# Normalisation split in two steps, a lagged mesh, and low weight parts made by accumulating DMAs

## The chip, the cores and the metric

One core of a Trainium2 chip runs the kernel. The metric is device microseconds of one execution. TensorE is called PE, VectorE DVE, ScalarE ACT, GpSimd POOL, and SyncE SP; SP issues all loads of the kernel before.

## The reference

Two transformer blocks over 512 tokens with a model width of 1024, in float32. Block 1 has two layers; block 2 has one, with a modulation computed from a vector c.

```python
for l in range(DEPTH):                                  # block 1, DEPTH = 2
    u = rmsnorm(x, norm_mix[l])
    proj = u @ w_in[l]
    q, k, v, iq, ik, iw, cB, cC, ch, g = jnp.split(proj, offsets, axis=-1)
    ...                                                 # rope on q, k, iq, ik
    y_attn = dsa_attention(q, k, v, iq, ik, iw) @ w_attn_out[l]
    y_conv = (cB * short_conv(cC * ch, conv_w[l])) @ w_conv_out[l]
    gates = jax.nn.sigmoid(g.reshape(B, T, N_BRANCH, D))
    merged = gates[:, :, 0] * y_attn + gates[:, :, 1] * y_conv
    x = x + merged @ w_mix_out[l]
    u = rmsnorm(x, norm_mlp[l])
    x = x + jnp.square(jax.nn.relu(u @ w_mlp_up[l])) @ w_mlp_down[l]
x = rmsnorm(x, norm_final)
mod = jax.nn.silu(c) @ w_ada[0] + b_ada[0]              # block 2
sh_m, sc_m, gt_m, sh_f, sc_f, gt_f = jnp.split(mod, N_MOD, axis=-1)
x = x + gt_m * token_mixer(modulate(rms_norm(x, g_mix), sh_m, sc_m), ...)
h = modulate(rms_norm(x, g_ffn), sh_f, sc_f)
x = x + gt_f * ((jax.nn.silu(h @ w_gate) * (h @ w_up)) @ w_down)
```

`dsa_attention` lets each query attend to the 128 keys of the highest index score; `token_mixer` joins a dilated attention with a chunkwise mLSTM.

## The kernel before, in words

Activations lie transposed, as eight tiles of 128 features by 512 tokens. Each float32 product is made of three float32r products: a value is split into a high part (`hi`) and the rest (`lo`), and hi x hi, hi x lo and lo x hi are summed in one PSUM bank. Activations are split by `hilo` and `prep`: ACT writes the high part, DVE subtracts it.

The program is a list of items that `Prog.run` walks in order. A "unit" is a piece of weights: 4 contraction tiles by 256 outputs (512 KB), or by 128 outputs where it is "narrow". Before the products of unit `cur` are emitted, the loads (`fetch`) of units up to `cur + early` (5) and the splits (`split`) of units up to `cur + ahead` (2) are emitted. `split` copies the raw weights to `wh` on ACT (L217) and subtracts into `wl` on DVE (L218); narrow units use slots of the general pool `gp` (62 of 128x512), the others four buffers of `whp`. There are eight raw buffers. "bg" items are background steps, taken out at a "rate" per unit, and "drain" empties them. The order in which each engine runs its instructions is set at build time and may differ a little from the order of the list.

`linear` makes products of 128 outputs by 512 tokens (L279 to L281), with `parts_=2` in two halves of 256 tokens. `linear_tok` makes V with the tokens as outputs (L430 to L432). `seven` makes a 2x2 block product in seven half-size products instead of eight (L401 to L403); it needs sums of weights (L327 to L336) and mixed activations `ta` and `tb`, which `mix` makes (L476 to L479, then `hilo` L455 and L456). `mesh` puts the pieces of one list between those of another, here the MLP's `down` of chunk c-1 between the `up` of chunk c.

A layer of block 1 runs: projections gC and gA, then V, q, k, H, B and the first gates, with the index scores and top-k (L795, L796) as background; `w_conv_out`; attention with the second gates; `w_attn_out`; `w_mix_out`, whose eviction `evmix` adds to x (L912), and prepares and squares the tile (L463, L464, L494, L495). The first MLP chunk u0 follows as a `linear`: after its second piece `rstd` sums the squares with a matrix of ones (L501), takes a root on ACT and a reciprocal on DVE over 128x512 (L503 to L505, `refine` L511 to L513), while four `mix` groups run as background; evictions are L928. Then the meshes follow, with c = 1 to 7, and the last `down`. Before the mixer, `norm` does the same `rstd` and `norm2` reduces its result to columns.

At the end of block 1 and before the FFN of block 2 the norm runs in column form, one half of the tokens after the other: `colsum` (L1045), a few instructions on two columns, `spread` (L1054 on DVE, L1056 on PE), and `hnorm` (L1066, L1076, L1079). The FFN begins with `gateup(0, 2)` and `gateup(1, 1)` in narrow units (L1533 to L1535).

Of the kernel before, what the change touches and what calls it, by code (L numbers as in the profile page):

```python
# [50 lines left out]
class Prog:  # L51
# [9 lines left out]
    def run(self):  # L61
        units = [p for k, p in self.items if k == "unit"]
        got = 0
        nxt = 0
        cur = 0
        bg = deque()
        rate = 1.0
        credit = 0.0
        for kind, pay in self.items:
            if kind == "unit":  # L70
                while got < len(units) and got <= cur + self.early:
                    self.fetch(units[got])
                    got += 1
                while nxt < len(units) and nxt <= cur + self.ahead:
                    self.split(units[nxt])
                    nxt += 1
                cur += 1
                credit += rate
                while credit >= 1.0:
                    credit -= 1.0  # L80
                    if bg:
                        bg.popleft()()
            elif kind == "do":
                pay()
            elif kind == "bg":
                bg.extend(pay)
            elif kind == "rate":
                rate = pay
            elif kind == "drain":
                while bg:  # L90
                    bg.popleft()()
# [18 lines left out]
def mesh(a, b):  # L110

    n = len(a)
    out = []
    for i, x in enumerate(a):
        out.extend(x)
        for p in b[i * len(b) // n : (i + 1) * len(b) // n]:
            out.extend(p)
    return out
# [3 lines left out]
def blocks_kernel(ctx: ExitStack, tc: tile.TileContext, a: dict, out: bass.AP, stop=None):  # L122
# [4 lines left out]
    xp = ctx.enter_context(tc.tile_pool(name="xp", bufs=1))  # L127
    gp = ctx.enter_context(tc.tile_pool(name="gp", bufs=62))
    bp = ctx.enter_context(tc.tile_pool(name="bp", bufs=1))
    rawp = ctx.enter_context(tc.tile_pool(name="rawp", bufs=8))  # L130
    whp = ctx.enter_context(tc.tile_pool(name="whp", bufs=4))
    ssp = ctx.enter_context(tc.tile_pool(name="ssp", bufs=2))
# [17 lines left out]
    def atbank():  # L150
        return atp.tile([P, T], F32, tag="at", name=nm("at"))
# [51 lines left out]
    def split(u):  # L203
# [13 lines left out]
        act.copy(hi, raw)  # L217
        dve.tensor_sub(lo, raw, hi.bitcast(F32))  # L218
        u["hi"], u["lo"] = hi, lo
# [16 lines left out]

    def linear(W, row0, kts, c0, widths, xs, evac, parts_=1, narrow=False, newbank=mmbank):

# [10 lines left out]
        steps = []  # L249
        kbase = 0  # L250
        for kt in kts:
            ch = chunk(W, row0 + kbase * P, kt, c0, cw)
            us = halves(ch, narrow)
            steps.append((kbase, kt, us))
            kbase += kt
# [154 lines left out]
    def linear_tok(W, c0, xs, evac):  # L410
# [26 lines left out]
        return pieces  # L437

    def add(pieces):
        for p in pieces:  # L440
            I.extend(p)
# [54 lines left out]

    def rstd(key):

        ps = atbank()
        with tc.issue_after(S["pe"].ins):  # L500
            pe.matmul(ps, ones, S[key, "ss"], start=True, stop=True)  # L501
        sd, v, rs = slot(), slot(), slot()
        act.activation(sd, ps, AF.Sqrt, bias=epsc, scale=1.0 / D)  # L503
        dve.tensor_scalar(v, ps, 1.0 / D, EPS, op0=ALU.mult, op1=ALU.add)
        dve.reciprocal(rs, sd)  # L505
        refine(rs, v, sd)
        S[key, "rs"] = rs

# [164 lines left out]
    def layer1(l, nextprep):  # L673
# [31 lines left out]
        def norm():  # L705
            rstd("n")
            rs = S["n", "rs"]
            dve.tensor_mul(S["Cr"], S["Cr"], rs)
            dve.tensor_mul(S["Sr"], S["Sr"], rs)

        def norm2():
            rs = S["n", "rs"]
            rs2 = slot()
            dve.tensor_mul(rs2, rs, rs)
            S["rs2"] = rs2
            rcol = small(NT, "rcol")
            for i in range(NT):
                junk = small(P, "junk")
                dve.scalar_tensor_tensor(
                    junk, rs[:, i * P : (i + 1) * P], 1.0, ident,  # L720
                    op0=ALU.mult, op1=ALU.mult, accum_out=rcol[:, i : i + 1],
                )
            S["rcol"] = rcol

# [13 lines left out]
        else:  # L738
            do(rope_tables)
            add(gC)  # L740
        gA = linear(W, 0, [4, 4], 1536, [P, P, 68], xs, evA)
        at = 1 if l else 3
        add(gA[:at])
        do(norm)
        add(gA[at:])
        do(norm2)


# [61 lines left out]

        gqk = linear_tok(W, 1024, xs, evv) + gq + gk
        LAG = 7
        add(gqk[:LAG])
        do(iwcols)
# [23 lines left out]

        add(linear(W, 0, [4, 4], 2884, [P] * 4, xs, evH))
        add(linear(W, 0, [4, 4], 1860, [P] * 4, xs, evB))  # L840

# [23 lines left out]
        for g in range(2):  # L865
            add(linear(W, 0, [4, 4], 4420 + 512 * g, [P] * 4, xs, evg1(g)))
        for g in range(2):
# [41 lines left out]
        def evmix(g):  # L909
            def f(j, ps, cs):  # L910
                j = 4 * g + j
                dve.tensor_add(x[j], ps, x[j])  # L912
                prep("n", j, col(C_NMLP + 8 * l + j))
            return f

        for g in range(2):
            add(linear(a["w_mix_out"][l], 0, [4, 4], 512 * g, [P] * 4, lambda k: m[k], evmix(g)))
        do(m.clear)
# [37 lines left out]

        def down(c):
            p = []
            last = c == NU - 1
            for g in range(2):  # L960
                p += linear(a["w_mlp_down"][l], 512 * c, [4], 512 * g, [P] * 4, lambda k: hid[4 * c + k], evdn(c, g),
                            parts_=2 if l == 1 and last and g == 1 else 1, narrow=not last, newbank=mmbank if last else atbank)

            def free():
                for k in range(4):
                    hid.pop(4 * c + k)

            p.append([("do", free)])
            return p
# [7 lines left out]

        def y(j):
            t = slot()
            act.activation(t, x[j], AF.Copy, scale=col(C_NMLP + 8 * l + j))  # L980
            return t

        u0 = linear(W_up, 0, [4, 4], 0, [P] * 4, xs, ev0)
        add(u0[:2])
        do(lambda: rstd("n"))
        I.append(("rate", 2.5))
        I.append(("bg", [f for k in range(4) for f in mix("n", k, y)]))
        add(u0[2:])
        I.append(("drain", None))
# [139 lines left out]
    def block2():  # L1129
# [364 lines left out]
        for g in range(2):  # L1494
            p = linear(a["w_out_2"], 0, [4, 4], 512 * g, [P] * 4, mx, evout(g), parts_=1 + g)
            if g == 0:
                p[2] = p[2] + [("do", mtail3)]
            add(p)
        do(O.clear)
# [233 lines left out]
```

## Time and profile before

| what | value |
|---|---|
| median of 3 runs | 2082.54 us (2080.67 to 2082.63) |
| the profiled execution | 2082.21 us, its span 2079.9 us |
| busy in the span | PE 2041.5, DVE 1575.5, ACT 982.9, POOL 19.5 us |
| DMA | 214.73 MB on SP's queue, 32.8% of 16 engines |

A busy engine is not one at its peak: products are pipelined, and the clock granted to PE changes. So the table of stretches is read for three things at once: PE's busy time, its granted clock, and what DVE and ACT do there.

### The profile page before, as it was taken

How to read it: one execution, taken by the hardware profiler on the slowest of the kernel's cores; microseconds unless marked ns; L12 is line 12 of the kernel's file. 1: busy time of each engine (PE TensorE's matmuls, PEld its weight loads, DVE VectorE, ACT ScalarE, POOL GpSimd, SP SyncE). 2: the span in 40 equal slices, each digit the busy share in tenths (PEclk: the TensorE clock that was granted, in tenths of full speed). 3: DMA queues.
4: the chain of work that ended last, by engine and by line, in shares of the span. 5: the costliest groups of instructions: out<-in, count | busy, mean ns of one | idle time of the engine just before them, and what ended most of it. 6: DMA issues, size and time to landing. Idle time of an engine off the chain costs nothing.

```text
span 2079.9 us, 29624 instructions
## 1 busy us (share of the span) xinstructions
PE 2041.5 (98%) x11552; PEld 1759.0 (85%) x11552; DVE 1575.5 (76%) x2801; ACT 982.9 (47%) x1699; POOL 19.5 (1%) x33
## 2 busy tenths in 40 slices
PE   9999999899999999999998999999999998999999
PEld 7888888799999878888886999998877787999998
DVE  6999666797877669977667888877777378777775
ACT  5324773544444432339545444445477744443442
POOL 0000000000000000000000000000000000000000
PEclk9999999999999999999998999999999999999999
DMA  7333212244444333331223444443321112233331
GB/s 233 96 97 101 72 62 92 91 142 142 145 160 142 102 97 92 101 102 53 78 84 104 144 148 152 153 132 91 92 72 62 51 61 82 92 102 104 100 100 42
DMA packets 199020, 216.60 MB, mean 104 GB/s; under 512 B 10721, under 2 KB 178017, under 8 KB 198881
## 3 DMA queue, kind: packets, MB, share of 16 engines
q1 hardware_dynamic: 198880, 214.73, 32.8%
q8 instruction: 90, 1.47, 0.3%
q14 instruction: 50, 0.40, 0.1%
HBM read 212.60 MB, written 2.10 MB: 103 GB/s over the span
## 4 chain that ended last, share of the span: by engine, by line
PE 91%; DVE 6%; ACT 2%; issue 1%; DMA 0%; POOL 0%; SPq 0%; DVEq 0%; ACTq 0%; POOLq 0%
PE mm L279 13%; PE mm L280 13%; PE mm L281 13%; PE mm L401 7%; PE mm L402 7%; PE mm L403 7%; PE at L279 7%; PE at L280 7%; PE at L281 7%; PE at L540 1%; PE ot L574 1%; PE mm L430 1%; PE mm L431 1%; PE mm L432 1%; PE at L559 1%
## 5 line engine op out<-in xcount | busy, mean ns | idle before, releaser
L217 ACT CAST wh<-raw 128x1024 fp32r<-128x1024 f32 (+3 forms) x272 | 277.5, 1024 | 537.0 <-PE mm L280 220.1
L279 PE MATMUL mm<-g,wh 128*128 128x512 f32 (+2 forms) x1328 | 506.9, 383 | 2.4 <-ACT g L1076 1.6
L281 PE MATMUL mm<-g,wl 128*128 128x512 f32 (+2 forms) x1328 | 503.4, 379 | 0.0
L280 PE MATMUL mm<-g,wh 128*128 128x512 f32 (+2 forms) x1328 | 502.4, 379 | 0.0
L218 DVE TENSOR_TENSOR wl<-raw,wh 128x1024 fp32r<-128x1024 f32 (+3 forms) x272 | 321.6, 1184 | 128.5 <-ACT wh L217 127.2
L401 PE MATMUL mm<-g,wh 128*128 128x256 f32 x1288 | 367.7, 285 | 14.9 <-DVE g L928 12.6
L402 PE MATMUL mm<-g,wh 128*128 128x256 f32 x1288 | 367.4, 285 | 1.0 <-DVE g L456 1.0
L403 PE MATMUL mm<-g,wl 128*128 128x256 f32 x1288 | 367.3, 285 | 0.0
L279 PEld LDWEIGHTS mm<-g,wh 128*128 128x128 f32 (+1 forms) x1328 | 250.1, 189 | 51.8 <-issue 4.3
L280 PEld LDWEIGHTS mm<-g,wh 128*128 128x128 f32 (+1 forms) x1328 | 250.1, 188 | 45.7 <-issue 1.2
L281 PEld LDWEIGHTS mm<-g,wl 128*128 128x128 f32 (+1 forms) x1328 | 250.0, 188 | 45.7
L401 PEld LDWEIGHTS mm<-g,wh 128*128 128x128 f32 x1288 | 250.1, 194 | 22.4 <-issue 8.9
L402 PEld LDWEIGHTS mm<-g,wh 128*128 128x128 f32 x1288 | 249.6, 194 | 7.0 <-DVE g L456 1.4
L403 PEld LDWEIGHTS mm<-g,wl 128*128 128x128 f32 x1288 | 249.6, 194 | 0.5
L279 PE MATMUL at<-g,g 128*128 128x512 f32 x608 | 239.7, 394 | 1.4 <-ACT g L455 1.4
L280 PE MATMUL at<-g,g 128*128 128x512 f32 x608 | 239.5, 394 | 0.1
L281 PE MATMUL at<-g,g 128*128 128x512 f32 x608 | 237.7, 391 | 0.0
L217 ACT CAST wh<-ws 128x1024 fp32r<-128x1024 f32 x69 | 72.4, 1050 | 216.0 <-PE mm L402 205.2
L281 PEld LDWEIGHTS at<-g,g 128*128 128x128 f32 x608 | 114.7, 189 | 24.8
L279 PEld LDWEIGHTS at<-g,g 128*128 128x128 f32 x608 | 115.2, 189 | 22.4 <-ACT g L455 3.0
L280 PEld LDWEIGHTS at<-g,g 128*128 128x128 f32 x608 | 115.2, 190 | 19.5 <-DVE g L456 0.9
L218 DVE TENSOR_TENSOR wl<-ws,wh 128x1024 fp32r<-128x1024 f32 x69 | 84.4, 1223 | 60.6 <-ACT wh L217 60.6
(265 smaller groups left out, 2716.7 us busy)
## 6 DMA issues: line engine op xcount, KB each, us to landing
raw<-w_in SPq DMA_DIRECT2D x111, 512.0 KB, 3.8
raw<-w_mlp_up SPq DMA_DIRECT2D x64, 512.0 KB, 3.8
raw<-w_mlp_down SPq DMA_DIRECT2D x64, 512.0 KB, 3.4
g<-w_ada SPq DMA_DIRECT2D x96, 256.0 KB, 4.2
raw<-w_gate SPq DMA_DIRECT2D x22, 512.0 KB, 3.6
raw<-w_up SPq DMA_DIRECT2D x22, 512.0 KB, 3.6
raw<-w_down SPq DMA_DIRECT2D x22, 512.0 KB, 3.4
raw<-w_mix_out SPq DMA_DIRECT2D x16, 512.0 KB, 3.4
```

Of the source, the lines that this page charges most:

```text
L217: act.copy(hi, raw)
L218: dve.tensor_sub(lo, raw, hi.bitcast(F32))
L279: pe.matmul(ps, wh, hi[:, cs], start=st, stop=False)
L280: pe.matmul(ps, wh, lo[:, cs], start=False, stop=False)
L281: S["pe"] = pe.matmul(ps, wl, hi[:, cs], start=False, stop=en)
L401: pe.matmul(ps, wh, hi, start=first and m == 0 and k == 0, stop=False, skip_group_check=True)
L402: pe.matmul(ps, wh, lo, start=False, stop=False, skip_group_check=True)
L403: S["pe"] = pe.matmul(ps, wl, hi, start=False, stop=k == 3, skip_group_check=True)
L430: pe.matmul(ps, xh, wh, start=kb + k == 0, stop=False)
L431: pe.matmul(ps, xl, wh, start=False, stop=False)
L432: pe.matmul(ps, xh, wl, start=False, stop=kb + k == KT - 1)
L540: pe.matmul(ps[:, :WM], qs[hh][:, i * P : (i + 1) * P], ks[hh][n][:, :WM], start=n == 0, stop=n == 1)
```

## The change

`rstd` becomes two steps in column form: `rstd1` (`colsum`, and the root on four columns) and `rstd2` (`spread`, and a copy). In layer 1 both run inside gC; `norm2` loses its column reductions. `w_mix_out`'s second half is made tile by tile (8 contraction tiles by 128 outputs per unit), and its evictions run `mix` for three of the four groups. `mesh` lags the second list by one piece of the first. The end of layer 1 joins the last two `down` chunks for the upper outputs in one product in two token halves. `ahead` and `early` become items of the list: (4, 7) from V to the first gates, (2, 5) after them; (5, 8) at the second half of `w_out_2`, (2, 5) at `gateup(1, 1)`. In the projections from V to the first gates, `adder` marks each unit: its `lo` is written by ACT as the negated high part, and a DMA issued from GpSimd adds the raw weights to it. `gp` goes from 62 to 56 slots, `whp` from 4 to 5 buffers, the DMA scratch from 256 to 4096.

```diff
@@ Prog.run
+            elif kind == "ahead":
+                self.ahead, self.early = pay
@@ mesh
-        for p in b[i * len(b) // n : (i + 1) * len(b) // n]:
-            out.extend(p)
+        if i:
+            for p in b[(i - 1) * len(b) // n : i * len(b) // n]:
+                out.extend(p)
+    for p in b[(n - 1) * len(b) // n :]:
+        out.extend(p)
@@ pools
-    gp = ctx.enter_context(tc.tile_pool(name="gp", bufs=62))
+    gp = ctx.enter_context(tc.tile_pool(name="gp", bufs=56))
-    whp = ctx.enter_context(tc.tile_pool(name="whp", bufs=4))
+    whp = ctx.enter_context(tc.tile_pool(name="whp", bufs=5))
@@ split
         act.copy(hi, raw)
-        dve.tensor_sub(lo, raw, hi.bitcast(F32))
+        if u.get("adder"):
+            act.activation(lo, raw, AF.Copy, scale=-1.0)
+            nc.gpsimd.dma_start(lo, raw, accum_op=ALU.add)
+        else:
+            dve.tensor_sub(lo, raw, hi.bitcast(F32))
@@ linear
+        if bytile:
+            ch = chunk(W, row0, total, c0, cw)
+            steps = [(0, total, [{"src": (ch, 0, total, c, P)}]) for c in range(0, cw, P)]
+            kts = []
@@ rstd
-    def rstd(key):
-        ps = atbank()
-        with tc.issue_after(S["pe"].ins):
-            pe.matmul(ps, ones, S[key, "ss"], start=True, stop=True)
-        sd, v, rs = slot(), slot(), slot()
-        act.activation(sd, ps, AF.Sqrt, bias=epsc, scale=1.0 / D)
-        dve.tensor_scalar(v, ps, 1.0 / D, EPS, op0=ALU.mult, op1=ALU.add)
-        dve.reciprocal(rs, sd)
-        refine(rs, v, sd)
-        S[key, "rs"] = rs
+    def rstd1(key):
+        ps, n = colsum([key], slice(0, T))
+        v, t, r = small(n, "m4"), small(n, "m4"), small(n, "rcol")
+        dve.tensor_scalar(v, ps[:, 0:n], EPS, None, op0=ALU.add)
+        act.activation(r, v, AF.Sqrt)
+        dve.reciprocal(r, r)
+        refine(r, v, t)
+        S["rcol"] = r
+    def rstd2(key):
+        ps = spread(S["rcol"], NT)
+        rs = S[key, "rs"] = slot()
+        act.copy(rs, ps)
@@ layer1, projections
+            add(gC[:3])                      # layer 1
+            do(lambda: rstd1("n"))
+            add(gC[3:6])
+            do(norm)
+            add(gC[6:])
...
-        gqk = linear_tok(W, 1024, xs, evv) + gq + gk
+        gqk = adder(linear_tok(W, 1024, xs, evv) + gq + gk)
+        I.append(("ahead", (4, 7)))
...
-        add(linear(W, 0, [4, 4], 2884, [P] * 4, xs, evH))
-        add(linear(W, 0, [4, 4], 1860, [P] * 4, xs, evB))
+        add(adder(linear(W, 0, [4, 4], 2884, [P] * 4, xs, evH)))
+        add(adder(linear(W, 0, [4, 4], 1860, [P] * 4, xs, evB)))
...
-            add(linear(W, 0, [4, 4], 4420 + 512 * g, [P] * 4, xs, evg1(g)))
+            add(adder(linear(W, 0, [4, 4], 4420 + 512 * g, [P] * 4, xs, evg1(g))))
+        I.append(("ahead", (2, 5)))
@@ layer1, evmix and the MLP
                 prep("n", j, col(C_NMLP + 8 * l + j))
+                if 4 <= j < KT - 1:
+                    for step in mix("n", j - 4, y):
+                        step()
...
-        add(u0[:2])
-        do(lambda: rstd("n"))
-        I.append(("rate", 2.5))
-        I.append(("bg", [f for k in range(4) for f in mix("n", k, y)]))
-        add(u0[2:])
+        add(u0[:1])
+        do(lambda: rstd1("n"))
+        I.append(("bg", mix("n", 3, y)))
+        add(u0[1:3])
+        do(lambda: rstd2("n"))
+        add(u0[3:])
...
-                I.extend(mesh(up(c), down(c - 1)))
+            if l == 1 and c == NU - 1:
+                I.extend(mesh(up(c), down(c - 1, (0,))))
+            else:
+                I.extend(mesh(up(c), down(c - 1)))
...
-        add(down(NU - 1))
+            add(down(NU - 1, (0,), last=True))          # layer 1
+            add(down(NU - 2, (1,), 2, last=True))
@@ block2
+                I.append(("ahead", (5, 8)))              # w_out_2, g = 1
...
+        I.append(("ahead", (2, 5)))
         add(gateup(1, 1))
```

## Rows read from the trace of the kernel before

**Rows 1.** The page: PE's part 1 row; its clock in 40 slices, in tenths.

```profile
PE 2041.5 (98%) x11552; PEld 1759.0 (85%) x11552; DVE 1575.5 (76%) x2801; ACT 982.9 (47%) x1699; POOL 19.5 (1%) x33
PEclk9999999999999999999998999999999999999999
```

**Rows 2.** Stretches: us, busy (x instructions) by engine, PE clock, DMA share, GB/s.

```profile
380.00:420.00 40.00, 32.37 (x158) 27.25 (x157) 31.27 (x53) 24.84 (x38) 0.00 (x0) 0.87 0.30 97
1100.00:1140.00 40.00, 30.21 (x150) 25.64 (x149) 29.06 (x48) 22.80 (x36) 0.00 (x0) 0.83 0.37 118
1420.00:1460.00 40.00, 35.60 (x257) 33.92 (x256) 32.47 (x93) 23.60 (x54) 0.00 (x0) 0.91 0.27 78
1720.00:1780.00 60.00, 52.58 (x315) 46.50 (x316) 51.83 (x95) 29.05 (x54) 0.00 (x0) 0.94 0.26 80
260.00:280.00 20.00, 19.13 (x126) 15.69 (x125) 13.28 (x36) 15.76 (x38) 1.67 (x2) 1.00 0.17 53
80.00:230.00 150.00, 150.00 (x667) 124.12 (x667) 134.96 (x258) 48.70 (x64) 1.22 (x2) 1.00 0.32 97
```

**Rows 3.** PE's waits in the whole span: us, times, longest.

```profile
PE mm L401 <- DVE g L928: 12.6, 4, 4.1
PE mm L1533 <- ACT g L217: 6.7, 3, 4.6
PE at L1056 <- DVE g L1054: 3.3, 3, 1.9
PE at L279 <- ACT g L455: 1.4, 2, 0.7
```

**Rows 4.** DVE groups, 366 to 406 us: count, busy us, mean ns, idle before.

```profile
L456 DVE TENSOR_TENSOR g<-g,g 128x512 fp32r<-128x512 f32 x9 | 6.1, 686 | 3.7 <-ACT g L455 3.7
L505 DVE RECIPROCAL g<-g 128x512 f32<-128x512 f32 x1 | 3.3, 3342 | 0.0
L476 DVE TENSOR_TENSOR g<-g 128x256 f32<-128x256 f32 x4 | 1.6, 402 | 0.0
L511 DVE TENSOR_TENSOR g<-g 128x512 f32<-128x512 f32 x1 | 0.7, 678 | 0.0
```

**Rows 5.** The stretch of w_mix_out's second half in layer 0.

```profile
344.00:366.00 22.00, 22.00 (x99) 18.22 (x98) 15.05 (x19) 9.32 (x14) 0.00 (x0) 1.00 0.31 96
```

**Rows 6.** Timeline of DVE at the block handover: start, us, what.

```profile
1445.97 0.16 DVE L1102 TENSOR_SCALAR n<-at 128x2 f32<-128x2 f32 x1 [2.86 <-PE at L1045]
1447.79 0.48 DVE L1054 TENSOR_SCALAR g<-kon,n 128x128 f32<-128x128 f32 x2
```

**Rows 7.** Timeline of PE at the block handover: start, us, what, wait.

```profile
1422.37 0.28 PE L279 MATMUL mm<-g,wh 128*128 128x256 f32 x1
1422.48 0.28 PE L280 MATMUL mm<-g,wh 128*128 128x256 f32 x1
1438.27 1.22 PE L279 MATMUL mm<-g,wh 128*128 128x256 f32 x4 [1.60 <-ACT g L1076]
1444.63 0.50 PE L1045 MATMUL at<-rdc,g 128*128 128x1 f32 x4
1448.41 1.19 PE L1056 MATMUL at<-g,kon 128*128 128x256 f32 x2 [1.89 <-DVE g L1054]
```

**Rows 8.** PE groups, 366 to 393 us: rstd's product with ones.

```profile
L501 PE MATMUL at<-g,kon 128*128 128x512 f32 x2 | 1.0, 592 | 0.0
```

**Rows 9.** Timeline of ACT at the FFN handover.

```profile
1726.06 2.16 ACT L217 CAST g<-raw 128x512 fp32r<-128x512 f32 x4
```

**Rows 10.** DVE groups in the projections of layer 0, 80 to 230 us.

```profile
L218 DVE TENSOR_TENSOR wl<-raw,wh 128x1024 fp32r<-128x1024 f32 x27 | 32.8, 1216 | 1.3 <-ACT wh L217 1.3
L801 DVE TENSOR_SCALAR bias<-g 128x512 f32<-128x512 f32 x1 | 0.4, 429 | 0.0
```

**Rows 11.** ACT's casts of weights in the same stretch.

```profile
L217 ACT CAST wh<-raw 128x1024 fp32r<-128x1024 f32 x27 | 28.4, 1051 | 70.5 <-PE mm L280 61.8 <-DVE g L521 4.4 <-issue 3.9
```

**Rows 12.** DMA issues: count, KB each, median us to landing.

```profile
raw<-w_in SPq DMA_DIRECT2D x111, 512.0 KB, 3.8
```

More of the change, by code (lines that the diff above doesn't have):

```diff
@@ L235, in halves, with linear @@
         return us
-    def linear(W, row0, kts, c0, widths, xs, evac, parts_=1, narrow=False, newbank=mmbank):
+    def linear(W, row0, kts, c0, widths, xs, evac, parts_=1, narrow=False, newbank=mmbank, bytile=False):
         pieces = []
@@ L437, in linear_tok, with adder @@
         return pieces
+    def adder(pieces):
+        for p in pieces:
+            for kind, u in p:
+                if kind == "unit":
+                    u["adder"] = True
+        return pieces
     def add(pieces):
@@ L705, in norm @@
         def norm():
-            rstd("n")
+            rstd2("n")
             rs = S["n", "rs"]
@@ L711, in norm2 @@
         def norm2():
-            rs = S["n", "rs"]
             rs2 = slot()
-            dve.tensor_mul(rs2, rs, rs)
+            dve.tensor_mul(rs2, S["n", "rs"], S["n", "rs"])
             S["rs2"] = rs2
[L716 to L723, printed above, removed]
         cc, cv, ycv = {}, {}, {}
@@ L739, in layer1 @@
             do(rope_tables)
-            add(gC)
-        gA = linear(W, 0, [4, 4], 1536, [P, P, 68], xs, evA)
[L742 to L745, printed above, removed]
+            add(gC[:3])
[3 more added lines that the diff above has]
+            add(gC[6:])
+        gA = linear(W, 0, [4, 4], 1536, [P, P, 68], xs, evA)
+        if l == 0:
+            add(gA[:1])
+            do(lambda: rstd1("n"))
+            add(gA[1:3])
+            do(norm)
+            add(gA[3:])
+        else:
+            add(gA)
         do(norm2)
@@ L913, in f, with y @@
                 prep("n", j, col(C_NMLP + 8 * l + j))
-            return f
+                if 4 <= j < KT - 1:
+                    for step in mix("n", j - 4, y):
+                        step()
+            return f
+        def y(j):
+            t = slot()
+            act.activation(t, x[j], AF.Copy, scale=col(C_NMLP + 8 * l + j))
+            return t
         for g in range(2):
-            add(linear(a["w_mix_out"][l], 0, [4, 4], 512 * g, [P] * 4, lambda k: m[k], evmix(g)))
+            add(linear(a["w_mix_out"][l], 0, [4, 4], 512 * g, [P] * 4, lambda k: m[k], evmix(g), bytile=g == 1))
         do(m.clear)
@@ L955, in up, with down @@
             return seven([(W_up, 512 * c), (W_up, 512 * c + 256)], xs, lambda k: S["n", "ta", k], lambda k: S["n", "tb", k], evup(c))
-        def down(c):
+        def down(c, gs=(0, 1), n=1, last=False):
             p = []
[L959 to L962, printed above, removed]
+            for g in gs:
+                p += linear(a["w_mlp_down"][l], 512 * c, [4] * n, 512 * g, [P] * 4, lambda k: hid[4 * c + k], evdn(c + n - 1, g),
+                            parts_=n, narrow=not last, newbank=mmbank if last else atbank)
             def free():
-                for k in range(4):
-                    hid.pop(4 * c + k)
-            p.append([("do", free)])
+                for k in range(4 * c, 4 * (c + n)):
+                    hid.pop(k)
+            if gs[-1]:
+                p.append([("do", free)])
             return p
@@ L976, in freen @@
                 S.pop(("n", "tb", k))
[L978 to L981, printed above, removed]
         u0 = linear(W_up, 0, [4, 4], 0, [P] * 4, xs, ev0)
-        add(u0[:2])
-        do(lambda: rstd("n"))
-        I.append(("rate", 2.5))
-        I.append(("bg", [f for k in range(4) for f in mix("n", k, y)]))
-        add(u0[2:])
+        add(u0[:1])
+        do(lambda: rstd1("n"))
+        I.append(("bg", mix("n", 3, y)))
+        add(u0[1:3])
+        do(lambda: rstd2("n"))
+        add(u0[3:])
         I.append(("drain", None))
@@ L993, in layer1 @@
         for c in range(1, NU):
-            I.extend(mesh(up(c), down(c - 1)))
+            if l == 1 and c == NU - 1:
+                I.extend(mesh(up(c), down(c - 1, (0,))))
+            else:
+                I.extend(mesh(up(c), down(c - 1)))
         do(freen)
@@ L999, in layer1 @@
             do(sqrt_table)
-        add(down(NU - 1))
+            add(down(NU - 1, (0,), last=True))
+            add(down(NU - 2, (1,), 2, last=True))
+        else:
+            add(down(NU - 1, last=True))
     modp = cp.tile([P, 2, 48], F32, name="modp")
@@ L1497, in block2 @@
                 p[2] = p[2] + [("do", mtail3)]
+            else:
+                I.append(("ahead", (5, 8)))
             add(p)
@@ L1723 @@
     from concourse.bass_utils import run_bass_kernel_spmd as _run
-    nc = _bacc.Bacc("TRN2", target_bir_lowering=False, num_devices=1, dynamic_dma_scratch_size=256)
+    nc = _bacc.Bacc("TRN2", target_bir_lowering=False, num_devices=1, dynamic_dma_scratch_size=4096)
     arrays = _pack(inputs)
```

## The prediction

> **What bounds the kernel now.** I read the page's first two parts first. TensorE (PE) is busy 2041.5 us, 98% of the span [rows 1], so a gain can come only from PE's own losses: 38.4 us of idle time out of 2079.9, and stretches at a lower granted clock. The clock row has 8 in one slice of forty and 9 in the others; the table of stretches finds the places [rows 2]. Where nothing is lost, as in the projections from 80 to 230 us, PE is at 150.00 of 150.00 us although VectorE (DVE) is at 135. The losses sit at four handovers, where one stage's output must be normalised or mixed before the next can start: 380 to 420 (layer 0, into the MLP), 1100 to 1140 (layer 1, the same), 1420 to 1460 (block 1 into block 2), 1720 to 1780 (block 2 into its FFN). Each loses idle time, plus the clock's shortfall times the stretch:
>
> - layer 0: 40 - 32.37 = 7.6 idle, 0.13 x 40 = 5.2 clock, 12.8 together
> - layer 1: 9.8 + 0.17 x 40 = 16.6
> - blocks: 4.4 + 0.09 x 40 = 8.0
> - FFN: 7.4 + 0.06 x 60 = 11.0
>
> Together 48.4 us: the ceiling of what handover changes can give. The list of PE's waits agrees: its longest are on L928, on L217's casts (at L1533) and on L1054, all there [rows 3]. The granted clock averaged 0.87 in the stretch that holds a wait of 4.1 us, so a part of it ran at the lower level, while 260 to 280 us, with 0.87 us idle, stayed at 1.00 [rows 2, 3]. Shrinking a long gap should return its clock loss too.
>
> **Layers 0 and 1, into the MLP.** By the DVE rows of the first MLP product [rows 4], `rstd` costs 3.34 (reciprocal, L505) and four 512-wide passes of 0.68 (L504 and the three refinements; the row of L511 stands for them), 6.1 us. Each of the four `mix` groups costs 4 x 0.41 (L476 to L479; the first stands) and 2 x 0.69 (L456), 3.0 us. They crowd in ahead of the evictions L928, for which PE waits 12.6 us in four waits over the two layers [rows 3].
> The change takes the reciprocal and its refinement to four columns: five instructions of 0.16 us and four 128-wide selects in `spread` at 0.24, by the rows on such operands in the block handover [rows 6]: 1.8 us, saving 4.3. It moves three mixes, 9.1 us of DVE, into the second half of `w_mix_out`, whose tiles now end 5.4 us apart (24 products at 0.225) instead of all late. That stretch has 22.0 - 15.05 = 6.95 us of idle DVE [rows 5], so about 2.2 us spills over. The relief of the first product is 4.3 + 9.1 - 2.2 = 11.2 us of DVE, against PE waits of 7.6 and 9.8. The lag in `mesh` hands `down` its operands one piece later, which covers the two small waits on L455 [rows 3]. What is late next: the sum of squares. `rstd1` now follows one piece (2.7 us) of the MLP product, not two, and the last tile's add, high part, low part and square (four passes of about 0.7, in series) come behind the spill. I leave a residue of 3 us in each layer (between 0 and 6): gains 9.8 and 13.6.
> On PE, `colsum` adds four one-column matmuls, 0.50 us [rows 7]; the spreading product replaces the ones product of 1.0 us [rows 8]. Two norms in two layers: a cost of 2.0 us. Layer 1's earlier norm inside gC, and the four column reductions gone from `norm2`, lie under a PE that is never idle there and give nothing.
>
> **Block 1 to 2.** The last two `down` chunks of the upper half of the outputs become one product in two token halves. A 256-wide product takes 0.12 from start to start [rows 7], so PE's second half lasts 96 x 0.12 = 11.5 us, not 5.8. From the start of the second half (1428.1, 48 such products after 1422.37) to the first product of block 2 (1438.3) the norm's chain took 10.2 us, which fits under it: the wait of 1.60 there goes, and the later one of 1.89 at the second norm follows, as its squares no longer queue behind the first half's `hnorm` [rows 7]. Forty-eight more products are cut in two halves, at 0.24 a pair for 0.225 whole: 0.7. With a residue of 1.3 the gain is 8.0 - 2.0 = 6.0.
>
> **FFN.** PE waits 4.6 us at L1533 for L217's casts of the gate and up weights [rows 3]; ACT runs four of them only at 1726.06, behind `hnorm` [rows 9]. With `ahead` 5 the casts of five narrow units stand in front of the second norm; each unit is 12 x 0.12 = 1.44 us of PE, 7.2 together, so the norm is covered but for a part. The other two of the three waits on these casts (6.7 - 4.6 = 2.1 us), before `gateup(1, 1)`, go by the same lead. Residue 2.5, gain 8.5.
>
> **The accumulating DMAs.** 28 units per layer (4 for V, 4 each for q, k, H and B, 8 for the gates), 56 in all. Each takes a DVE subtraction of 1.22 us away [rows 10], adds an ACT pass like the cast's 1.05 [rows 11], and a 512 KB SBUF-to-SBUF DMA on GpSimd's queue. DVE's 34 us per layer are worth nothing, since PE does not wait in that stretch, and ACT has 150 - 48.7 = 101 us idle for 29 more [rows 2]. The waits added: GpSimd waits for ACT's negated copy, with only the next such DMAs and the few `kl` copies behind it; ACT's cast waits for one of five `wh` buffers, as it waits now for one of four (61.8 us idle on L280 [rows 11]), with the evictions of the same unit behind it, which PE has yet to produce; SP's loads wait for raw buffers, held until the DMA has read them.
> *Latency.* At 150/28 = 5.36 us per unit, four units ahead leave 21.4 - 2.1 = 19.3 us for the DMA. A 512 KB load lands in 3.8 us [rows 12], so five times that would still fit. Only the first unit of a layer is split two units ahead, some 8 us, of which ACT takes 2.1: a wait from 0 to 3 us per layer. I take 0.5 each, near the load's row: 1.0.
> *Throughput.* The trace has no accumulating DMA. The nearest row is the load: 0.32 of all engines in this stretch [rows 2], 1.7 us per unit for one read and one write. With a second read, three passes for two, I estimate 2.6 us (bounds 1.7 and, at four times, 6.9). 1.7 + 2.6 = 4.3, under 5.36. The cost I take is nothing; the cover ends at 3.65 us per DMA.
>
> The Trainium skill speaks against this placement: "SBUF — State Buffer", section "Who interferes with whom", says that DMAs issued from GpSimd need it to write descriptors through a port that DVE locks in its two-port modes, which `copy`, `cast` and `tensor_scalar` can enter. By that rule, were every DVE instruction to lock, the DMAs would run only in DVE's gaps; the same list takes `tensor_tensor`'s writes out of it.
>
> **Sum.** Gains 9.8 + 13.6 + 6.0 + 8.5 = 37.9; costs 2.0 + 1.0; net 34.9. The profiled execution took 2082.21 us, 2.3 of it around the span, against a median of 2082.54; 2082.2 - 34.9 = 2047.3. By its own bounds: no residues at all, 2036; residues doubled (+9.8) and 3 us at each layer's first unit (+5), 2062.
>
> **Rivals.**
> *The accumulating DMAs bind PE* (slower). Past 3.65 us of all engines per 512 KB, loads and DMAs together outlast a unit. Past 4.27 us the 34.9 are eaten (0.62 x 56). At three times the load, 5.1 us, 1.7 + 5.1 - 5.36 = 1.4 per unit, 81 us, gives 2128; at four times some 2225. For it: the DMA engines are a third busy already. Against it: three passes for two is half more, not twice. Chance 0.12. A narrow band of it (2078 to 2087) is no change.
> *DVE starves GpSimd* (slower). If GpSimd could prepare a DMA only in DVE's idle time, 15 us of 150 for 28 DMAs, or 0.54 us each, and one took 1 us of it, units would come every 10 us: 4.6 x 56 more, 2305 us. Against it: the stretch's largest group is TENSOR_TENSOR; TENSOR_SCALAR from SBUF is three instructions, of which the row of L801 is the longest, 0.43 [rows 10]. Chance 0.03. (It is the mechanism that the Trainium skill describes at the place named.)
> *New waits take the old ones' place.* PE waits at `colsum` in both layers for about 4 us, the size beside which the clock fell. With clock loss in the proportion of layer 0 (5.2 to 7.6), 2.7 each, 13 us come back, less the 6 of the residues: 2055; with the block and FFN residues doubled too, 2058. For it: DVE has no slack left in the second half of `w_mix_out`. Chance 0.11.
> *The smaller pool* (56 slots for 62) delays casts in the MLP loops. Of 19 meshes, one wait of 0.7 us (the size of the two on L455) in one or two places of each: 13 to 27, 2060 to 2074. Against it: these loops lose nothing now, and reuse needs one narrow unit ahead. Chance 0.08.
>
> **How the numbers follow.** The forecast, 2036 to 2062, has 0.66. The rivals of new waits and of the pool stay faster. The two DMA rivals hold 0.15, of which 0.03 falls within 0.2% (about what a measurement of this kernel can tell from no change) and 0.12 is slower. Since the operation that decides is in no row, I move 0.03 from faster to slower: 0.82, 0.03, 0.15. The range, 2035 to 2080, takes in the forecast and the two middle rivals and leaves out some 0.18.
>
> **What would show it.** Right: no PE wait over 1.5 us and a clock of 1.00 in the layers' handovers; the first product of block 2 without a wait on L1076; PE at 150 of 150 in the projections, with DVE 33 us lower, a DMA share of 0.7 to 0.85, and the accumulating DMAs landing within 8 us. Wrong: PE waiting for a DMA in the projections, a DMA share near 1, or a landing over 19 us; PE waiting at `colsum` with the clock low; waits on L455 or L217 inside the meshes. Had the change done nothing at the handovers, the waits of rows 3 would stand, and the time with them.

## The result and the profile after

The changed kernel takes 2061.89 us (median of 4 runs, 2061.23 to 2062.91) against 2082.59 for the kernel before in the same job: ratio 0.9902, 95% interval 0.9885 to 0.9919. It is 20.7 us faster, where 34.9 were forecast. The spans of the two profiled executions, 2079.9 and 2060.3 us, differ by 19.6, so the profile holds nearly all of it.

The page of the changed kernel: TensorE (PE) and the other engines, and the queue of the accumulating DMAs (packets, MB, share of 16 engines).

```profile
PE 2037.2 (99%) x11632; PEld 1757.5 (85%) x11632; DVE 1497.1 (73%) x2739; ACT 1035.0 (50%) x1757; POOL 67.1 (3%) x89
q0 software_dynamic: 8064, 29.36, 7.7%
```

The table of stretches of the changed kernel (length, busy time and instructions of PE, its weight loads, DVE, ACT and GpSimd, then PE's clock, DMA share, GB/s). The FFN handover starts 20 us earlier than before, so its stretch is moved. The last five lines are places where the prediction counted no loss, or a small one.

```profile
380.00:420.00 40.00, 40.00 (x239) 35.59 (x238) 32.82 (x47) 22.36 (x34) 0.00 (x0) 1.00 0.37 119
1100.00:1140.00 40.00, 40.00 (x250) 36.12 (x249) 34.56 (x59) 19.19 (x32) 0.00 (x0) 1.00 0.54 175
1420.00:1460.00 40.00, 38.65 (x266) 34.70 (x265) 32.85 (x78) 20.51 (x44) 0.00 (x0) 1.00 0.36 104
1700.00:1760.00 60.00, 53.36 (x311) 47.10 (x310) 49.60 (x90) 28.06 (x51) 0.00 (x0) 0.91 0.25 79
80.00:230.00 150.00, 150.00 (x668) 124.13 (x667) 110.78 (x224) 64.36 (x80) 16.70 (x20) 1.00 0.70 166
420.00:710.00 290.00, 287.02 (x1748) 256.96 (x1748) 227.66 (x373) 126.03 (x205) 0.00 (x0) 1.00 0.45 140
1140.00:1400.00 260.00, 256.76 (x1604) 232.30 (x1603) 205.42 (x337) 115.20 (x187) 0.31 (x1) 0.99 0.44 139
1240.00:1300.00 60.00, 57.76 (x350) 51.83 (x349) 47.98 (x80) 24.69 (x42) 0.00 (x0) 0.97 0.44 140
820.00:840.00 20.00, 20.00 (x90) 16.58 (x89) 19.66 (x46) 6.03 (x6) 2.61 (x3) 1.00 0.94 205
```

The same stretches of the two layers' MLP loops in the kernel before:

```profile
420.00:710.00 290.00, 290.00 (x1792) 261.75 (x1791) 233.18 (x383) 126.71 (x209) 0.00 (x0) 1.00 0.44 141
1140.00:1420.00 280.00, 280.00 (x1741) 253.21 (x1740) 223.00 (x372) 121.69 (x202) 0.31 (x1) 1.00 0.44 142
```

Beside [rows 2]: the two layers' handovers, 7.6 and 9.8 us idle at 0.87 and 0.83 before, are full at 1.00. Blocks 1 to 2 keep 1.35 us idle, at 1.00. The FFN kept its idle time (6.6 for 7.4) and its clock fell further (0.91 for 0.94). And the MLP loops, where PE had no idle time at all, now lose 3.0 and 3.2 us idle, and in layer 1 some clock. The list of PE's waits (us, times, longest), to be read against [rows 3]:

```profile
PE at L295 <- DVE g L228: 6.1, 8, 2.2
PE mm L1574 <- ACT g L1115: 2.8, 1, 2.8
PE mm L1574 <- ACT g L222: 2.6, 3, 1.5
PE at L1095 <- DVE g L1093: 1.3, 2, 1.2
```

The evictions L928 (12.6 us before) are gone from it. In their place the first line stands for DVE's narrow weight subtractions in the MLP loops; the second is the norm's second part at the FFN.

Why do subtractions come late in the loops? There `w_ada`, the weights of block 2's modulation, is loaded and multiplied as a background job: each load takes a slot of `gp`, and DVE multiplies what it brought. First DVE's waits for these loads (layer 0, then layer 1), then the waits of SP, which issues them, for a free slot, in the changed kernel:

```profile
DVE g L1056 <- DMA g<-w_ada: 26.5, 14, 4.1
DVE g L1056 <- DMA g<-w_ada: 19.4, 13, 4.6
SPq L1055 <- DVE g L978: 27.7, 9, 6.5
SPq L1055 <- PE at L295: 17.5, 19, 2.6
SPq L1055 <- DVE g L1056: 10.6, 3, 4.3
```

Before, the two DVE waits were 1.4 us in 3 and 2.4 us in 3. One instance on the timelines (start, us, what, wait) of SP, DVE and PE; the second line is from the chain of work that ended last:

```profile
1256.02 3.28 SPq L1055 DMA_DIRECT2D g<-w_ada  x2
1256.02 5.93 DMA g<-w_ada
1261.97 0.69 DVE L1056 SCALAR_TENSOR_TENSOR g<-g,g 128x512 f32<-128x512 f32 x1 [4.56 <-DMA g<-w_ada]
1264.33 0.69 DVE L228 TENSOR_TENSOR g<-raw,g 128x512 fp32r<-128x512 f32 x1
1265.08 0.80 PE L295 MATMUL at<-g,g 128*128 128x512 f32 x1 [2.24 <-DVE g L228]
```

The first load goes out as a product of PE frees its slot, and takes 5.93 us to land. The second follows after a wait of 2.5 us for a slot. DVE stands 4.56 us at the operation that needs the first. The narrow subtraction that PE needs is queued behind, and PE stops for 2.24 us. The clock of 1240 to 1300 is 0.97, of the loop before 1.00.

### The profile page after: what moved, and what is told of

Read it like the earlier page. It is cut to its first block, busy times and chain, and to the rows that moved or that the text cites. A ratio compares the mean times of both kernels' runs of the same rounds, so it can differ in the third digit from the quotient of the medians.

```text
span 2060.3 us, 29994 instructions
## 1 busy us (share of the span) xinstructions
PE 2037.2 (99%) x11632; PEld 1757.5 (85%) x11632; DVE 1497.1 (73%) x2739; ACT 1035.0 (50%) x1757; POOL 67.1 (3%) x89
## 4 chain that ended last, share of the span: by engine, by line
PE 88%; DVE 6%; DMA 3%; ACT 1%; issue 1%; SPq 0%; POOL 0%; DVEq 0%; ACTq 0%; POOLq 0%
PE mm L293 14%; PE mm L294 13%; PE mm L295 13%; PE mm L416 6%; PE mm L415 6%; PE mm L417 6%; PE at L295 6%; PE at L293 6%; PE at L294 6%; DMA g<-w_ada 2%; PE at L566 2%; PE mm L444 1%; PE mm L445 1%; PE mm L446 1%; PE at L585 1%; PE ot L600 1%
## 5 line engine op out<-in xcount | busy, mean ns | idle before, releaser
L222 ACT CAST wh<-raw 128x1024 fp32r<-128x1024 f32 (+3 forms) x274 | 279.2, 1023 | 484.2 <-PE mm L416 202.3
L293 PE MATMUL mm<-g,wh 128*128 128x512 f32 (+1 forms) x1360 | 514.2, 379 | 0.7 <-ACT wh L222 0.6
L295 PE MATMUL mm<-g,wl 128*128 128x512 f32 (+1 forms) x1360 | 512.3, 377 | 0.0
L294 PE MATMUL mm<-g,wh 128*128 128x512 f32 (+1 forms) x1360 | 511.7, 376 | 0.0
L228 DVE TENSOR_TENSOR wl<-raw,wh 128x1024 fp32r<-128x1024 f32 (+2 forms) x218 | 256.1, 1177 | 109.2 <-ACT wh L222 108.3
L293 PEld LDWEIGHTS mm<-g,wh 128*128 128x128 f32 x1360 | 255.1, 188 | 49.7 <-issue 4.1
L295 PEld LDWEIGHTS mm<-g,wl 128*128 128x128 f32 x1360 | 255.4, 188 | 46.1 <-issue 0.7
L294 PEld LDWEIGHTS mm<-g,wh 128*128 128x128 f32 x1360 | 255.4, 188 | 45.4 <-issue 1.0
L415 PEld LDWEIGHTS mm<-g,wh 128*128 128x128 f32 x1288 | 246.9, 192 | 4.9
L416 PEld LDWEIGHTS mm<-g,wh 128*128 128x128 f32 x1288 | 246.7, 192 | 4.8
L417 PEld LDWEIGHTS mm<-g,wl 128*128 128x128 f32 x1288 | 246.7, 192 | 0.0
L295 PE MATMUL at<-g,g 128*128 128x512 f32 x592 | 232.1, 392 | 6.2 <-DVE g L228 6.1
L293 PE MATMUL at<-g,g 128*128 128x512 f32 x592 | 232.5, 393 | 0.0
L294 PE MATMUL at<-g,g 128*128 128x512 f32 x592 | 232.3, 392 | 0.0
L222 ACT CAST wh<-ws 128x1024 fp32r<-128x1024 f32 x69 | 72.4, 1049 | 183.8 <-PE mm L416 159.8
L295 PEld LDWEIGHTS at<-g,g 128*128 128x128 f32 x592 | 111.6, 188 | 32.8 <-DVE g L228 9.0
L293 PEld LDWEIGHTS at<-g,g 128*128 128x128 f32 x592 | 112.1, 189 | 19.8
L294 PEld LDWEIGHTS at<-g,g 128*128 128x128 f32 x592 | 112.0, 189 | 18.9
```

The lines of the kernel that those rows point to most:

```text
L293: pe.matmul(ps, wh, hi[:, cs], start=st, stop=False)
L294: pe.matmul(ps, wh, lo[:, cs], start=False, stop=False)
L295: S["pe"] = pe.matmul(ps, wl, hi[:, cs], start=False, stop=en)
L415: pe.matmul(ps, wh, hi, start=first and m == 0 and k == 0, stop=False, skip_group_check=True)
L416: pe.matmul(ps, wh, lo, start=False, stop=False, skip_group_check=True)
L417: S["pe"] = pe.matmul(ps, wl, hi, start=False, stop=k == 3, skip_group_check=True)
```

## The experiments

My theory after the result: the accumulating DMAs are neutral; the smaller pool costs about 10 us in the MLP loops through the `w_ada` loads; the FFN part gains nothing because the longer lead (five units split ahead of PE instead of two) queues later work ahead of the norm. Rivals: the lag in `mesh` makes the loss, or the accumulating DMAs do.

Ratios and intervals are against the kernel before in the same job. Where times of two jobs are compared, the kernel before took 2082.34 to 2083.66 us in them, so such a difference is open by about 1 us.

**1. The pool, the lag and the accumulating DMAs.** Four kernels in one job (before: 2082.63).

No accumulating DMAs:

```diff
-                    u["adder"] = True
+                    u["adder"] = False
-        I.append(("ahead", (4, 7)))
```

> The changed kernel with the accumulating DMAs taken out (low parts by DVE's subtraction again, units split two ahead in the projections as before); the pool stays at 56 slots. Theory, the accumulating DMAs are neutral: 2062, within 4. Rival, they cost time that the trace hides (a shared DMA ring, later loads): under 2056. Rival, they gain something: over 2066.

Measured: 2064.08 us (ratio 0.9911, 0.9897 to 0.9925). Against 0.9902 (0.9885 to 0.9919) of the whole change this is not told apart from nothing: with this pool, the accumulating DMAs are neutral.

The same, and the memory that they had taken given back:

```diff
-    gp = ... bufs=56    whp = ... bufs=5    dynamic_dma_scratch_size=4096
+    gp = ... bufs=62    whp = ... bufs=4    dynamic_dma_scratch_size=256
```

> As the run before it, and the memory that the accumulating DMAs needed given back: 62 slots in the pool, four weight buffers, the small DMA scratch. Only the handover changes are left. Pool theory (the meshes lose 10 us because loads of w_ada wait for slots): 2052, within 4, and DVE's waits for w_ada loads in the meshes back to a few us. Rival, the lag in mesh holds buffers longer and makes the loss: 2062, as the run before it.

Measured: 2050.98 us (0.9848, 0.9834 to 0.9861), 13.1 us better. The loops and DVE's waits in them in this kernel:

```profile
420.00:710.00 290.00, 289.75 (x1772) 260.66 (x1771) 230.24 (x377) 126.43 (x208) 0.00 (x0) 1.00 0.45 141
1140.00:1400.00 260.00, 260.00 (x1652) 236.80 (x1651) 207.24 (x346) 115.43 (x192) 0.31 (x1) 1.00 0.44 140
DVE g L1055 <- DMA g<-w_ada: 2.6, 3, 1.5
DVE g L1055 <- DMA g<-w_ada: 3.2, 7, 0.9
```

PE is full again but for 0.25 us, and the waits for `w_ada` are back near their size of before. The weight buffers and the scratch changed with the pool; that the pool counts is shown only by what the loops wait for, the slots.

The small pool in the kernel before:

```diff
-    gp = ctx.enter_context(tc.tile_pool(name="gp", bufs=62))
+    gp = ctx.enter_context(tc.tile_pool(name="gp", bufs=56))
```

> The kernel before with 56 slots instead of 62 and nothing else. Pool theory: 2082.5 + 10 = 2092, within 5, with DVE waiting some 40 us for w_ada loads in the two layers' meshes. Rival, the lag: 2082.5, within 3.

Measured: 2078.05 us (0.9978, 0.9969 to 0.9987), not slower but 4.6 us faster. So the small pool alone costs nothing: neither the pool theory nor the lag's 2082.5 is met. Yet SP waits longer for slots here than in the changed kernel:

```profile
SPq L1016 <- PE at L281: 77.2, 24, 6.5
```

DVE waits for `w_ada` only 11.4 us in 9 and 3.3 us in 7, and the loops keep PE full (290.00 of 290.00 and 260.00 of 260.00 us). So a slot that comes late is not enough: it costs only where the load then lands after DVE has reached the operation that needs it. Here most of the wait is for slots that PE frees; in the changed kernel the largest part is for slots that DVE itself frees (L978). That this makes the difference is not shown.

The changed kernel with the mesh of before:

```diff
-        if i:
-            for p in b[(i - 1) * len(b) // n : i * len(b) // n]:
-                out.extend(p)
-    for p in b[(n - 1) * len(b) // n :]:
-        out.extend(p)
+        for p in b[i * len(b) // n : (i + 1) * len(b) // n]:
+            out.extend(p)
```

> The changed kernel with the mesh of before (the down pieces not lagging by one). Pool theory: 2062 to 2064, the small waits on L455 of before (1.4 us) come back and the mesh loss stays. Lag theory: 2052, the mesh loss goes.

Measured: 2054.39 us (0.9865, 0.9851 to 0.9878), 7.5 us better than the whole change. Its loops:

```profile
420.00:710.00 290.00, 288.89 (x1765) 259.42 (x1764) 230.60 (x377) 127.68 (x211) 0.00 (x0) 1.00 0.45 139
1140.00:1400.00 260.00, 259.30 (x1645) 235.64 (x1645) 206.04 (x343) 114.63 (x191) 0.31 (x1) 1.00 0.45 141
```

They lose 1.1 and 0.7 us, and DVE waits for `w_ada` 11.1 and 12.3 us: between the 5.8 us in all of the kernel with 62 slots and the 45.9 of the changed kernel. The small waits on L455 did not come back. So most of the loss takes both: with the lag, 56 slots (with the buffers and the scratch) cost 13.1 us; at 56 slots, the lag costs 7.5; the small pool without lag and without the other edits costs nothing. The changed kernel with 62 slots and no lag was not run. That the lag holds the `hid` pairs of a chunk for longer, and so leaves fewer free slots, fits this but is argued from the code.

**2. Is it the loads of `w_ada`?** The changed kernel, its loads left out:

```diff
-                nc.sync.dma_start(w, a["w_ada"][...])
-                dve.scalar_tensor_tensor(w, w, 1.0, S["cb", n2], ...)
+                dve.scalar_tensor_tensor(w, S["cb", n2], 0.0, S["cb", n2], ...)
```

> The changed kernel with the loads of w_ada in the meshes left out; DVE's operations of the same length stay and take the same slots, on data that is there (the modulation is then its bias alone). Theory, the meshes lose their time because DVE stands in order behind loads that got a slot late: 2052, within 2, PE's waits on L228 in the meshes nearly gone. Rival, the lack of slots holds up the casts themselves: 2060 or more.

Measured: 2051.88 us (0.9847, 0.9832 to 0.9861), 10.0 us better, as the theory said (2052). This kernel leaves the loads out, so its modulation is the bias alone. Its loops:

```profile
420.00:710.00 290.00, 290.00 (x1768) 260.89 (x1767) 231.65 (x376) 128.34 (x210) 0.00 (x0) 1.00 0.34 101
1140.00:1400.00 260.00, 260.00 (x1657) 236.92 (x1656) 205.01 (x345) 114.65 (x193) 0.31 (x1) 1.00 0.33 102
```

With 56 slots, the lag, and the same DVE work, PE is full. So the slots suffice for casts and products, and the loss comes through the loads. That it goes through DVE, standing in order behind a late load, is what the waits and the instance above show. The run itself would not tell this from two other effects of the same edit: without the loads a slot is held for less time, and SP has less to issue in front of the weights.

**3. What opened the layers' handovers.** Both on the kernel of 2050.98 us (handover changes alone, 62 slots). The mixes back in the first product:

```diff
-                if 4 <= j < KT - 1:
-                    for step in mix("n", j - 4, y):
-                        step()
...
-        I.append(("bg", mix("n", 3, y)))
         add(u0[1:3])
         do(lambda: rstd2("n"))
+        I.append(("rate", 2.5))
+        I.append(("bg", [f for k in range(4) for f in mix("n", k, y)]))
```

> The handover changes alone with 62 slots, with the four mixes of each layer back in the first MLP product, as in the kernel before; the norm by columns and all else stay. By the prediction's split, the mixes are 6.9 of the 11.2 us of DVE relief in each layer: some 60% of the 30 us that the two layers' handovers gave back is lost, 2051 + 18 = 2069, between 2062 and 2076. Rival, the shorter norm alone opens the handover: 2051 to 2055.

Measured: 2081.12 us (0.9993, 0.9984 to 1.0002). All 30 us are gone, more than the 18 expected and outside the bounds. PE's longest waits, and the first handover:

```profile
PE mm L415 <- ACT g L477: 11.2, 4, 5.2
PE mm L415 <- DVE g L959: 7.5, 2, 3.9
380.00:420.00 40.00, 29.70 (x140) 25.23 (x139) 28.31 (x48) 23.83 (x36) 0.00 (x0) 0.79 0.25 79
```

PE now waits for the mixed operands themselves (L477), and the stretch is worse than before (10.3 us idle at 0.79 for 7.6 at 0.87). My edit starts the mixes a piece later than the kernel before did, so its 30 us is an upper bound of what moving them is worth.

The full-width norm back, mixes still moved:

```diff
-        add(u0[:1])
-        do(lambda: rstd1("n"))
+        add(u0[:2])
+        do(lambda: rstd("n"))
         I.append(("bg", mix("n", 3, y)))
-        add(u0[1:3])
-        do(lambda: rstd2("n"))
-        add(u0[3:])
+        add(u0[2:])
```

> The handover changes alone with 62 slots (2051 before this edit), with the MLP's norm in the two layers as in the kernel before (ones product, reciprocal and refinement over 512 columns), and the mixes still moved into w_mix_out's second half. By the prediction's split the norm by columns is 4.3 of the 11.2 us of DVE relief in each layer: PE's waits at the evictions come back in part, about 4.3 us a layer and the clock loss beside them, 2051 + 12 = 2063, between 2058 and 2068. Rival, the moved mixes alone open the handover: 2050 to 2053.

Measured: 2061.38 us (0.9892, 0.9876 to 0.9909), 10.4 us lost, within the expected bounds. Its two handovers:

```profile
380.00:420.00 40.00, 36.07 (x205) 31.64 (x204) 31.21 (x45) 20.90 (x32) 0.00 (x0) 0.91 0.36 114
1100.00:1140.00 40.00, 36.63 (x213) 32.44 (x213) 31.18 (x51) 19.68 (x33) 0.00 (x0) 0.91 0.48 158
```

3.9 and 3.4 us idle, and 0.09 x 40 = 3.6 of clock in each: most of the 4.3 us of DVE a layer that the prediction gave the norm by columns comes back as idle time, with the clock's share on top. By these rows 14.5 us would be lost, where the run lost 10.4; the difference is open. The two shares, 30 and 10 us, add up to more than the 30 that the two edits gained together, so they are not separate prices.

**4. The FFN.** All on the kernel of 2050.98 us, in which this stretch reads:

```profile
1690.00:1750.00 60.00, 53.37 (x322) 47.80 (x322) 50.00 (x96) 27.55 (x51) 0.00 (x0) 0.94 0.23 71
1703.34 1.23 DVE L341 TENSOR_TENSOR ws<-raw,raw 128x1024 f32<-128x1024 f32 x1 [2.19 <-DMA raw<-w_up]
1709.89 1.65 DVE L1104 SCALAR_TENSOR_TENSOR g<-x,gf,at 128x256 f32<-128x256 f32 x4
```

The two timeline lines are DVE's: a sum for a later unit waits 2.19 us for its load, and the norm's second part (L1104 on DVE, then L1114 on ACT) runs behind it. On ACT two casts for later units, held up by such a sum, also stand in front of L1114. PE waits 2.8 us for it, until 1711.5.

Without the longer lead:

```diff
-            else:
-                I.append(("ahead", (5, 8)))
```

> The handover changes alone with 62 slots, without the longer lead at the FFN (two units, as in the kernel before). Theory, that part of the change gains nothing as it stands: 2051, within 2. Rival, it gains the 8.5 us of the prediction and another part of the change loses them: 2059.

Measured: 2055.19 us (0.9869, 0.9856 to 0.9883). The lead is worth 4.2 us by the medians, though the intervals overlap a little: between the two theories. The stretch in this kernel, with the wait of 4.6 us on the casts back:

```profile
1690.00:1750.00 60.00, 51.77 (x289) 44.98 (x288) 50.43 (x95) 26.95 (x50) 0.00 (x0) 0.89 0.27 79
PE mm L1571 <- ACT g L222: 6.4, 3, 4.6
```

With the lead ended as the first gate and up product begins:

```diff
         u0 = gateup(0, 2)
+        I.append(("ahead", (2, 5)))
         add(u0[:8])
```

> The handover changes alone with 62 slots (2051 before this edit), and the lead of splits set back to two units as the first gate and up product begins, so that the five splits made ahead of the norm stay but no later ones are queued in front of the norm's second part. Theory, the FFN's new wait of 2.8 us on L1114 comes from DVE's later splits and sums (one of them waits 2.2 us for a load of w_up) queued ahead of it: that wait goes with the clock loss beside it, 2046, within 2. Rival, the handover is bound by the chain of norms itself: 2051, within 1.

Measured: 2051.65 us (0.9851, 0.9838 to 0.9865): no gain. The wait on L1114 is gone (0.2 us are left) as predicted, but PE waits 4.5 us in 5 for casts (L222), in place of 2.4 in 3. My theory named the wait rightly, and not what would take its place.

With the lead, and the norm's second part four pieces earlier:

```diff
-        add(u0[:8])
+        add(u0[:4])
         do(lambda: S.pop("rest")())
-        add(u0[8:])
+        add(u0[4:])
```

> The handover changes alone with 62 slots and the longer lead kept at the FFN, but the norm's second part of the second half of the tokens is queued four pieces earlier, ahead of the splits of the later units. Theory, the FFN needs both, the early casts and the norm in time: the wait of 2.8 us on L1114 goes and the casts stay early, with the clock loss beside them 2046, within 2. Rival, ACT and DVE have so much to do in this stretch that the wait moves on to the casts: 2051, within 1.5.

Measured: 2048.16 us (0.9831, 0.9816 to 0.9846), the fastest of all kernels here; 2.8 us below its base, just outside what was expected, with intervals that overlap, so a gain is likely but not shown by the times. The stretch and the waits that are left in it:

```profile
1690.00:1750.00 60.00, 54.38 (x347) 48.58 (x346) 52.79 (x97) 30.72 (x55) 0.00 (x0) 1.00 0.28 80
PE mm L1573 <- ACT g L222: 2.0, 3, 0.9
PE mm L1573 <- ACT g L1581: 1.9, 1, 1.9
```

Idle time fell by 1.0 us only, and the clock is at 1.00 for 0.94 (3.6 us).

Two pieces earlier instead of four (`u0[:6]`, `u0[6:]`):

> As the run before it (2048), with the norm's second part queued two pieces early instead of four, so that the two Silu evictions of the first half of the tokens stand ahead of it on ACT. Theory, the run before was held for 1.9 us by a Silu (L1581, with its table load) behind the norm's part, and this order loses neither: 2046, within 1.5. Rival, the wait on L1114 comes back in its place: 2048 to 2051.

Measured: 2049.89 us (0.9842, 0.9828 to 0.9855), not told apart from the run before. L1581 is not waited for and L1114 for 0.2 us, but the casts (L222) take 3.9 us in 4. The rival's time, by neither's mechanism: in this stretch the waits move between ACT's casts, its Silus and the norm.

**5. The accumulating DMA at double the work.**

```diff
-    gp = ... bufs=56
+    gp = ... bufs=54
...
             nc.gpsimd.dma_start(lo, raw, accum_op=ALU.add)
+            nc.gpsimd.dma_start(lo, zero[...], accum_op=ALU.add)
```

> The changed kernel with a second accumulating DMA behind each of the 56, which adds a tile of zeros (two slots of the pool are given for it). By the estimate from the page of the changed kernel, 7.7% of 16 engines for 56 DMAs, one takes 2.8 us of all engines; two and the load take 1.7 + 5.6 = 7.3 us where PE needs 5.36 for a unit, so PE is bound by the DMAs in the projections and loses 1.9 x 56 = 109 us: 2170, between 2130 and 2190. Rival, the DMA engines overlap these transfers better than the share of time says: under 2090.

Measured: 2237.78 us (1.0744, 1.0729 to 1.0759), worse than expected, by another limit. Most of it lies in the projections (151.91 of 200 us busy in the stretch below): the two slots fewer cost the MLP loops only some 3 us of idle time more. GpSimd's waits and the stretch, from 80 to 280 us; then the DMAs (count, KB, median us from issue to landing):

```profile
POOL wl L229 <- DMA wl<-raw: 159.8, 21, 10.3
80.00:280.00 200.00, 151.91 (x553) 117.04 (x551) 99.96 (x216) 54.36 (x62) 35.94 (x41) 0.88 0.81 172
wl<-raw POOLq DMA_DIRECT2D x56, 512.0 KB, 8.4
wl<-zero POOLq DMA_DIRECT2D x56, 512.0 KB, 6.5
```

The second DMA adds to the same tile, so GpSimd waits in order until the first has landed, and the next unit's first DMA is queued behind that wait. A unit takes about 9.2 us here (the second DMAs are issued 9.2 us apart on average), near the first DMA's landing of 8.4, while the DMA engines are at 0.81, not 1. So this run priced the landing time in series. (The wait is needed: the Trainium skill, "DMA: Bandwidth & Descriptors", section "Rules for kernel authors", says of accumulating DMAs that a second write to the same bytes must await the first one's semaphore; no run here leaves the wait out.) The throughput at which the DMAs would bind PE was not measured.

## Why the prediction was right or wrong

The direction and the range held; the point was 14.6 us too low. That the time still lies inside the forecast's own bounds, 2036 to 2062, is partly luck: two steps failed by 9.5 and 8 to 10 us, and residues that did not come gave 6 of it back. By its terms, gains as positive:

- **Layers 0 and 1**: forecast 9.8 and 13.6, measured 12.8 and 16.6 (the whole ceilings of [rows 2]). The mechanism was right, and experiment 3 shows that both parts were needed. The mis-sized step is the residue of 3 us a layer: nothing was left, no wait at `colsum` appeared there, and the rival of new waits did not occur.
- **Blocks 1 to 2**: forecast 6.0. By rows 8.0 - 1.35 = 6.65, less the 0.7 for halves: 6.0. The wait at L1095 (1.2 us) is the residue.
- **FFN**: forecast 8.5. By rows 11.0 before, and 6.6 + 0.09 x 60 = 12.0 after: -1.0. The step that failed is "the norm is covered but for a part": it counted the lead's casts in front of the norm, and not that the lead stays on through the product, so that later splits and sums stand in front of the norm's second part, one of them waiting for a load (2.8 us of PE's time). The lead alone is worth about 4 us (2055.2 to 2051.0); ending it early only moved the waits to the casts (experiment 4).
- **The MLP loops**: forecast nothing; the covered waits on L455 were the only entry for the lag. By rows 3.0 idle in layer 0, and 3.2 idle with 0.03 x 60 = 1.8 of clock in layer 1: 8.0; by leaving the loads out, 10.0. The failed step is the argument against the smaller pool, "reuse needs one narrow unit ahead": it looked at weight slots alone, when the loads of `w_ada` take slots from the same pool and DVE waits for them in order. The rival had 0.08, and the time fell into its 2060 to 2074. It too named the wrong partner: casts, where it was DVE's queue, and the pool alone, where it takes the lag.
- **Accumulating DMAs**: forecast nothing but 1.0 for the first units; neutral in the first experiment. The estimate of 2.6 us of all engines measured 0.077 x 2060.3 / 56 = 2.8, so 1.7 + 2.8 = 4.5 us a unit, under 5.36. They landed in 6.3 us (sign: within 8), the share in 80 to 230 us was 0.70, PE 150.00. DVE was 24 us lower there, not 33, for only 18 of the 27 units in that stretch were such (nine subtractions of other weights stand in it). Landing is longer than a unit, yet with four units ahead there is time for it, and several can be on the way at once: the cover that the run with two in series took away. The wait at a layer's first unit (1.0 in all) did not come: PE's whole list has no wait for these DMAs.
- **`colsum`**: forecast 2.0. Before, its products were 3.3 us of busy time (24 of them), after 7.4 (below): twice the price, since four columns are eight instructions, and [rows 7] shows the four of two columns.

```profile
L1084 PE MATMUL at<-rdc,g 128*128 128x1 f32 x56 | 7.4, 245 | 0.5 <-DVE g L517 0.4
wl<-raw POOLq DMA_DIRECT2D x56, 512.0 KB, 6.3
```

The sum: 34.9 + 6.0 (layers) - 9.5 (FFN) - 8.0 (loops) - 2.1 (`colsum`) + 1.0 (first units) = 22.3, for 19.6 in the spans; the 2.7 left is in none of these rows. With the 10.0 us of experiment 2 for the loops, in place of 8.0, the sum is 20.3.

The two slower rivals did not come. DVE did not starve GpSimd: from 820 to 840 us DVE is busy 19.66 of 20.00 us, the DMA engines 0.94, and PE 20.00. The rule of the Trainium skill weighed there ("SBUF — State Buffer", section "Who interferes with whom") is not tested by that: of the operations that it names as able to enter the two-port modes, this stretch holds one TENSOR_SCALAR of 0.35 us.

## What to carry to other kernels

When an edit pays for a gain with buffers, list every user of that pool, side jobs too, and ask who waits in order behind each. A load that gets its buffer late costs nothing by itself; it costs when an engine needed by others waits for it at the head of its queue. Two edits that look free each by itself (fewer slots, operands held longer) are to be priced together. And a neutral part of a change is not free if it was paid for in memory: without the accumulating DMAs, and with their memory given back, the same handover edits reach 2051 us instead of 2062.

## What was not expected of the hardware

The same waits went with different granted clocks. In the kernel before with 56 slots, PE's waits on L928 are the same 12.6 us in 4 (longest 4.1) as in [rows 3], and layer 1's handover (5 us earlier) is as full as in [rows 2], yet at 0.91 for 0.83:

```profile
PE mm L401 <- DVE g L928: 12.6, 4, 4.1
1095.00:1135.00 40.00, 30.16 (x160) 25.66 (x159) 31.21 (x53) 24.08 (x38) 0.00 (x0) 0.91 0.38 126
```

0.08 x 40 = 3.2 us, most of the 4.6 by which that kernel was faster; layer 0's handover has 0.91 for 0.87 as well. Why it was so stays open. At the FFN, too, two kernels with a longest wait of 4.6 us on the casts show 0.94 (before, 7.4 us idle) and 0.89 (without the lead, 8.2 us idle). So a clock loss taken in proportion to idle time, as the prediction took it, is good to some 3 us a handover here.
